# Running sums of the later modulation, 1024 columns wide, and the second gate in the first stream

## The chip, the cores and the metric

The kernel runs on one core of one Trainium2 chip. The metric is the device time of one execution in microseconds (us): the median of the runs shown, 1925.47 us. The profile is of one execution, and its own times are counted from the first to the last instruction (the span). The engines are TensorE (PE, whose weight loads are listed as PEld), VectorE (DVE), ScalarE (ACT), GpSimd (POOL) and SyncE (SP, which here issues nearly all DMAs).

## The reference

Two layers over a sequence of 512 rows with 2048 features, all in float32. Each layer is modulated by a conditioning vector `c`:

```python
c_act = silu(c)
for l in range(2):
    shift, scale, gate = split(c_act @ w_mod[l] + b_mod[l], 3)
    h = x * (1 + scale) + shift
    if l == 0:                       # differential attention, 8 heads, ALiBi
        y = diff_attention(h, a_w_in, a_w_out, ...)
    else:                            # forgetting attention, 16 heads
        sh, sc = split(c_act @ kv_w_mod + kv_b_mod, 2)
        k, v, zf = split((x * (1 + sc) + sh) @ kv_w, ...)
        F = cumsum(log_sigmoid(zf + b_f))
        y = forgetting_attention(h, b_w_in, b_w_out, k, v, F)
    x = layer_norm(ALPHA * x + gate * y, ln_g[l], ln_b[l])
```

`w_mod[l]` is 2048 x 6144 and `kv_w_mod` 2048 x 4096. So beside the large products there are vector-matrix products whose weights must all be read once: shift and scale of layer 0, its gate, shift and scale of the shared keys and values, and shift, scale and gate of layer 1.

## The kernel before

**Matmuls.** A float32 product is made of three TensorE products of a high and a low part (`products`, lines 208 to 210). The weights come as tiles of 128 x 2 x 512 (`wst`), are cast on ACT to the high part (`whi`, L113), and DVE subtracts to get the low part (`wlo`, L114). `WeightStream` loads them up to four tiles ahead and has two or three split tiles ready. A `group` is one job of 512 output columns: 8 weight tiles, and for each of them 4 bursts (one for each of four accumulators in PSUM) of 6 matmuls. After the last weight tile each accumulator is evicted by ACT and DVE (`evac`), and the next group takes the same four accumulators. Jobs come in this order: the start (the first heads, under an order written out by hand), then for heads 2 to 7 a query/key group (`qk`) and a value/gate group (`vg`), the output projection of layer 0 (`oA`, 4 groups), the shared values (`vj`, 5 groups), the shared keys (`kj`, 4 groups), layer 1's query/gate groups, and its output projection. What stands in `pieces` (attention of the head before, built from small closures) is taken up one piece per burst, in `tick`.

**The sums.** The vector-matrix products of the later modulation are not made on TensorE. DVE keeps a running sum: for each block of 128 rows, `macc = w * cact + macc` over 512 columns (L433; the first block L431), with `cact` as a scalar for each partition. After 16 blocks the sum still has to be added over the 128 partitions: a 32 x 32 transpose (L464) and a reduction (L465) on DVE, and once for each vector a small matmul (L474), an add of the bias, and a store to DRAM.

**Background and ticks.** The generator `mod_stream` makes one step of a sum for each `next`. `tick` calls it after a burst as often as the group's `bg` says. So the spread of ticks over bursts sets how densely the sums stand among the other work. There are two streams:

- the first (pool `ap`): gate of layer 0 (4 segments of 512 columns) and the shared keys' and values' shift and scale (8 segments). Each load is 128 x 2 x 512, 512 KB, two steps' worth, in two buffers. It runs from group `qk[2]` to `vg[7]`.
- the second (pool `npool`, made in `open_n`): shift and scale (8 segments) and gate (4 segments) of layer 1. Each load is 128 x 512, 256 KB, in three buffers, and steps 50 to 105 use tiles of the pool `kpool` and are loaded 8 ahead. It runs in groups 1 and 2 of `oA`, in `vj[1]` to `vj[4]` and in all of `kj`.

The results come back through DRAM: `fold(0)` in the first group of `oA`, `fold(1)` 9 bursts into `kj[2]`, and the gates are broadcast (`row_bcast`) in the output projections.

**Order.** After the start, a planner gives each engine its list of instructions at build time, from its own costs and from the dependencies; the steps of the sums are kept in program order among themselves. Each engine then works through its list in order, and so does the DMA queue of SP.

Of the kernel before, what the change touches and what calls it, by code (L numbers as in the profile page):

```python
# [10 lines left out]
F32 = mybir.dt.float32  # L11
# [3 lines left out]
ALU = mybir.AluOpType  # L15

P = 128
D = 2048
# [126 lines left out]
def tile_yoco(  # L145
# [250 lines left out]
    def mod_stream(segs, new_stage, new_acc, nk, deep=range(0), new_deep=None):  # L396

        todo = [(i, r) for i in range(len(segs)) for r in range(KT // nk)]  # L400
        loaded = {}
        summed = []

        def load(k):
            i, r = todo[k]
            src, col, _ = segs[i]
            t = new_deep() if k in deep else new_stage()
            rows = src[nk * r * P : nk * (r + 1) * P, col : col + 512]
            nc.sync.dma_start(t, rows.rearrange("(k p) n -> p k n", p=P) if nk > 1 else rows)
            loaded[k] = t  # L410

        def load_upto(k):
            n = len(loads)
            while n < len(todo) and n <= (k + 7 if n in deep else k + 2 // nk):
                load(n)
                loads.append(n)
                n += 1

        loads = []
        load_upto(-1)  # L420
        for k, (i, r) in enumerate(todo):
            load_upto(k)
            if r == 0:
                acc = new_acc()
            t = loaded.pop(k)
            for kk in range(nk):
                kt = nk * r + kk
                w = t[:, kk, :] if nk > 1 else t

                if kt == 0:  # L430
                    ins = V.tensor_scalar(acc, w, cact[:, 0:1], None, op0=ALU.mult)  # L431
                else:
                    ins = V.scalar_tensor_tensor(acc, w, cact[:, kt : kt + 1], acc, op0=ALU.mult, op1=ALU.add)  # L433
                tc.keep_in_program_order(ins)
                if kt == KT - 1:
                    summed.append(segs[i][2](acc))
                if kt in (1, 9) and summed:
                    if next(summed[0], None) is None:
                        summed.pop()
                yield  # L440
        for n, _ in enumerate(summed[0]):

            for _ in range(1 if n else 6):
                yield
# [375 lines left out]
    segs = []  # L820
    fours = four_ones(ap)
    for dst, src, col, bias, one in (
        (gate_dram[0], w_mod[0], 2 * D, b_mod[0], (0.0,)),
        (mod_dram[0], kv_w_mod, 0, kv_b_mod, (0.0, 1.0)),
    ):
        n = len(one)
        steps = mod_rows(ap, fours, dst, bias[col : col + n * D], one)
        segs += [(src, col + 512 * f, partial(steps, f)) for f in range(4 * n)]
    background = mod_stream(
        segs,  # L830
        lambda: ap.tile([P, 2, 512], F32, name="ms", tag="ms", bufs=2),
        lambda: ap.tile([P, 512], F32, name="macc", tag="macc", bufs=2),
        2,
# [264 lines left out]
    group(qk[2], False, lambda b, acc: keep(("qk", b), acc), bg=lambda k: k % 3 == 2)  # L1098
# [41 lines left out]
    group(vg[2], True, keep_vg, bg=lambda k: k % 2)  # L1140
    for h in range(3, A_HEADS):
# [16 lines left out]
        group(qk[h], False, evac, bg=lambda k: k % 2)  # L1158
# [11 lines left out]
        group(vg[h], True, evac_rest, bg=lambda k: 1 if k % 8 in (1, 3, 4, 5, 7) else 0, after_sub=early if h == A_HEADS - 1 else None)  # L1170
# [17 lines left out]
    def out_projection(jobs, layer, zp, opened, residual, norm, after_held=None):  # L1188
# [10 lines left out]
        for k, (f, job, banks) in enumerate(jobs):  # L1199
# [54 lines left out]
            bg = (lambda n: 1 if n % 3 else 0) if layer == 0 and k in (1, 2) else 0  # L1254
# [7 lines left out]
    def open_n():  # L1262
        nonlocal background
        actx.close()
        pool = nctx.enter_context(tc.tile_pool(name="npool", bufs=1, reuse_waits="tile"))
        zp.extend((pool, pool.tile([P, TB, D], F32, name="n"), pool.tile([P, TB, 4, 6], F32, name="nstats")))
        fours = four_ones(pool)
        segs = []
        for dst, col, one in ((mod_dram[1], 0, (0.0, 1.0)), (gate_dram[1], 2 * D, (0.0,))):
            n = len(one)  # L1270
            steps = mod_rows(pool, fours, dst, b_mod[1, col : col + n * D], one)
            segs += [(w_mod[1], col + 512 * f, partial(steps, f)) for f in range(4 * n)]
        background = mod_stream(
            segs,
            lambda: pool.tile([P, 512], F32, name="ms", tag="ms", bufs=3),
            lambda: pool.tile([P, 512], F32, name="macc", tag="macc", bufs=2),
            1,

            deep=range(50, 106),
            new_deep=lambda: ktile("msk"),  # L1280
        )
# [560 lines left out]
```

## Time and profile before

| | |
|---|---|
| runs of the kernel | 1925.35, 1925.47, 1926.13 us |
| span of the profiled execution | 1923.5 us, 2.0 us below the median of the runs (its time with what lies around the span is not listed) |
| PE busy | 1910.4 us (99%), 8921 matmuls |
| DVE busy | 1370.3 us (71%) |
| ACT busy | 732.9 us (38%) |
| granted TensorE clock | 0.999 |
| DMA | 382.22 MB, mean 199 GB/s |
| steps of the sums on DVE (L433, L431) | 360 and 24, 512 columns each |
| loads of the sums issued on SP (L409) | 168 + 64 + 56 |

How to read it: "busy" is the time in which an engine has work in hand, as a share of the span. Matmuls overlap, so each is listed with 0.39 us while in the chain of waits one follows the other after 0.23 us. In the lists a tile is named by its program name (`macc<-ms,cact,macc`), L433 is line 433 of the kernel, and what stands after `<-` in brackets or behind a bar is what ended an engine's idle time.

### The profile page before, as it was taken

How to read it: one execution, taken by the hardware profiler on the slowest of the kernel's cores; microseconds unless marked ns; L12 is line 12 of the kernel's file. 1: busy time of each engine (PE TensorE's matmuls, PEld its weight loads, DVE VectorE, ACT ScalarE, POOL GpSimd, SP SyncE). 2: the span in 40 equal slices, each digit the busy share in tenths (PEclk: the TensorE clock that was granted, in tenths of full speed). 3: DMA queues.
4: the chain of work that ended last, by engine and by line, in shares of the span. 5: the costliest groups of instructions: out<-in, count | busy, mean ns of one | idle time of the engine just before them, and what ended most of it. 6: DMA issues, size and time to landing. Idle time of an engine off the chain costs nothing.

```text
span 1923.5 us, 25879 instructions
## 1 busy us (share of the span) xinstructions
PE 1910.4 (99%) x8921; PEld 1593.5 (83%) x8921; DVE 1370.3 (71%) x2617; ACT 732.9 (38%) x1266; POOL 2.3 (0%) x11
## 2 busy tenths in 40 slices
PE   8999999999999999999999999999999999999998
PEld 7888888888888888888888898888888888888887
DVE  8993578777676868667675477777566666686768
ACT  3656344333232344521272232224344444453122
POOL 0000000000000000000000000000000000000000
PEclk9999999999999999999999999999999999999999
DMA  9993566676767675476557586775355555555622
GB/s 346 385 333 95 160 186 196 213 234 196 228 203 224 207 223 180 122 241 222 179 165 256 181 294 211 258 258 160 114 149 156 161 149 160 154 154 170 224 93 110
DMA packets 352275, 382.22 MB, mean 199 GB/s; under 512 B 77912, under 2 KB 256244, under 8 KB 351376
## 3 DMA queue, kind: packets, MB, share of 16 engines
q1 hardware_dynamic: 349040, 376.23, 62.2%
q10 hardware_dynamic: 3104, 4.35, 0.6%
q8 instruction: 70, 1.15, 0.3%
q14 instruction: 61, 0.50, 0.1%
HBM read 348.68 MB, written 31.80 MB: 198 GB/s over the span
## 4 chain that ended last, share of the span: by engine, by line
PE 97%; DVE 1%; SPq 1%; DMA 0%; issue 0%; ACT 0%; ACTq 0%
PE acc L208 27%; PE acc L210 27%; PE acc L209 27%; PE acc L720 4%; PE sc L720 2%; PE sc L210 1%; PE sc L209 1%; PE sc L208 1%; PE o L208 1%; PE o L210 1%; PE o L209 1%; PE o L720 1%; SPq L568 0%; PE tr L686 0%; PE tr L660 0%; DMA sms<-in_w_mod_dram 0%
## 5 line engine op out<-in xcount | busy, mean ns | idle before, releaser
L113 ACT CAST whi<-wst 128x1024 fp32r<-128x1024 f32 (+2 forms) x298 | 303.4, 1018 | 617.6 <-PE acc L210 310.1
L114 DVE TENSOR_TENSOR wlo<-wst,whi 128x1024 fp32r<-128x1024 f32 (+2 forms) x298 | 351.4, 1180 | 248.8 <-ACT whi L113 228.9
L208 PE MATMUL acc<-hh,whi 128*128 128x512 f32 x1184 | 462.9, 391 | 0.0
L209 PE MATMUL acc<-hl,whi 128*128 128x512 f32 x1184 | 461.6, 390 | 0.0
L210 PE MATMUL acc<-hh,wlo 128*128 128x512 f32 x1184 | 460.0, 390 | 0.0
L208 PE MATMUL acc<-whi,hh 128*128 128x512 f32 (+1 forms) x1104 | 418.5, 379 | 0.0
L209 PE MATMUL acc<-wlo,hh 128*128 128x512 f32 (+1 forms) x1104 | 416.7, 377 | 0.0
L210 PE MATMUL acc<-whi,hl 128*128 128x512 f32 (+1 forms) x1104 | 416.2, 377 | 0.0
L433 DVE SCALAR_TENSOR_TENSOR macc<-ms,cact,macc 128x512 f32<-128x512 f32 x307 | 229.0, 746 | 63.0 <-DMA ms<-in_w_mod_dram 44.5
L210 PEld LDWEIGHTS acc<-hh,wlo 128*128 128x128 f32 x1184 | 222.3, 188 | 47.4
L208 PEld LDWEIGHTS acc<-hh,whi 128*128 128x128 f32 x1184 | 222.3, 188 | 44.0 <-DVE sgb L1509 0.8
L209 PEld LDWEIGHTS acc<-hl,whi 128*128 128x128 f32 x1184 | 222.5, 188 | 42.3
L210 PEld LDWEIGHTS acc<-whi,hl 128*128 128x128 f32 x1104 | 207.3, 188 | 38.9
L208 PEld LDWEIGHTS acc<-whi,hh 128*128 128x128 f32 x1104 | 207.3, 188 | 37.2 <-DVE ztmp L1241 0.6
L209 PEld LDWEIGHTS acc<-wlo,hh 128*128 128x128 f32 x1104 | 207.4, 188 | 36.0
L618 DVE SCALAR_TENSOR_TENSOR sacc<-sms,cact,sacc 128x512 f32<-128x512 f32 (+1 forms) x128 | 89.9, 703 | 4.6 <-DMA sms<-in_w_mod_dram 0.7
L904 ACT ACTIVATE e<-e,mn 128x128 f32<-128x128 f32 (+3 forms) x64 | 36.0, 563 | 109.5 <-DVE mn L900 102.9
L1559 ACT ACTIVATE eb<-eb,mnb 128x128 f32<-128x128 f32 (+1 forms) x64 | 35.9, 561 | 72.7 <-DVE mnb L1556 72.4
L720 PE MATMUL acc<-wlo,hh 128*128 128x512 f32 x128 | 49.8, 398 | 0.0
L720 PE MATMUL acc<-whi,hl 128*128 128x512 f32 x128 | 49.3, 393 | 0.0
L720 PE MATMUL acc<-whi,hh 128*128 128x512 f32 x128 | 49.2, 393 | 0.0
L132 DVE TENSOR_TENSOR wlo<-wst,whi 128x768 fp32r<-128x768 f32 (+1 forms) x32 | 34.8, 1088 | 17.8 <-ACT whi L125 16.5
(336 smaller groups left out, 2096.6 us busy)
## 6 DMA issues: line engine op xcount, KB each, us to landing
wst<-in_a_w_in_dram SPq DMA_DIRECT2D x240, 256.0 KB
ms<-in_w_mod_dram SPq DMA_DIRECT2D x136, 256.0 KB
ms<-in_kv_w_mod_dram SPq DMA_DIRECT2D x64, 512.0 KB
wst<-in_b_w_in_dram SPq DMA_DIRECT2D x128, 256.0 KB
sms<-in_w_mod_dram SPq DMA_DIRECT2D x56, 512.0 KB
wst<-in_kv_w_dram SPq DMA_DIRECT2D x56, 512.0 KB
ms<-in_w_mod_dram SPq DMA_DIRECT2D x32, 512.0 KB
wst<-in_a_w_out_dram SPq DMA_DIRECT2D x32, 512.0 KB
```

What stands on the lines that cost most here:

```text
L113: self.nc.scalar.copy(hi[:, :, :w], st[:, :, :w])
L114: self.nc.vector.tensor_tensor(lo[:, :, :w], st[:, :, :w], hi[:, :, :w].bitcast(F32), op=ALU.subtract)
L132: self.nc.vector.tensor_tensor(lo[:, :, :w], st[:, :, :w], hi[:, :, :w].bitcast(F32), op=ALU.subtract)
L208: PE.matmul(dst, lhs[0], rhs[0], start=start, stop=False, skip_group_check=True)
L209: PE.matmul(dst, lhs[0], rhs[1], start=False, stop=False, skip_group_check=True)
L210: PE.matmul(dst, lhs[1], rhs[0], start=False, stop=stop, skip_group_check=True)
L433: ins = V.scalar_tensor_tensor(acc, w, cact[:, kt : kt + 1], acc, op0=ALU.mult, op1=ALU.add)
L618: V.scalar_tensor_tensor(acc, w, sc, acc, op0=ALU.mult, op1=ALU.add)
L720: PE.matmul(bank[n, bk], l, r, start=start, stop=stop, skip_group_check=True)
L904: S.activation(e[:, :w], e[:, :w], AF.Exp, bias=mn, scale=-1.0, accum_out=rs)
L1559: S.activation(e[:, :w], e[:, :w], AF.Exp, bias=mn, scale=-1.0, accum_out=rs)
```

## The change

- `mod_stream` now works on 1024 columns with one accumulator and one 512 KB load (128 x 1024) per step, two buffers, one load ahead; the deep prefetch is gone. After a segment's 16 steps come two steps of their own for the two transposes and reductions; five empty steps stand before the last vector's matmul.
- Layer 1's gate moves from the second stream to the first, between layer 0's gate and the shared shift and scale.
- The ticks (`bg`) are spread anew in each group.

```diff
-    def mod_stream(segs, new_stage, new_acc, nk, deep=range(0), new_deep=None):
...
+    def mod_stream(segs, new_stage, new_acc, ahead):
+
+        todo = [(i, kt) for i in range(len(segs)) for kt in range(KT)]
+        loaded, turned_sums = [], []
 
         def load_upto(k):
...
+            while len(loaded) < min(k + 1, len(todo)):
+                i, kt = todo[len(loaded)]
+                src, col, _ = segs[i]
+                loaded.append(new_stage())
+                nc.sync.dma_start(loaded[-1], src[kt * P : (kt + 1) * P, col : col + 1024])
+
+        for k, (i, kt) in enumerate(todo):
+            load_upto(k + ahead)
+            w, one = loaded[k], cact[:, kt : kt + 1]
+            loaded[k] = None
+            if kt == 0:
                 acc = new_acc()
...
+                ins = V.tensor_scalar(acc, w, one, None, op0=ALU.mult)
+            else:
+                ins = V.scalar_tensor_tensor(acc, w, one, acc, op0=ALU.mult, op1=ALU.add)
+            tc.keep_in_program_order(ins)
+            if kt == 4:
+                while turned_sums:
+                    next(turned_sums.pop(0), None)
+            yield
+            if kt == KT - 1:
+                for half, steps in enumerate(segs[i][2]):
+                    turned_sums.append(steps(acc[:, 512 * half : 512 * half + 512]))
+                    next(turned_sums[-1])
+                    yield
+        for _ in range(5):
+            yield
+        for steps in turned_sums:
+            next(steps, None)
...
     background = mod_stream(
...
+        vectors(
+            ap, (
+                (gate_dram[0], w_mod[0], 2 * D, b_mod[0], (0.0,)), (gate_dram[1], w_mod[1], 2 * D, b_mod[1], (0.0,)),
+                (mod_dram[0], kv_w_mod, 0, kv_b_mod, (0.0, 1.0)),
+            ),
+        ),
+        lambda: ap.tile([P, 1024], F32, name="ms", tag="ms", bufs=2),
+        lambda: ap.tile([P, 1024], F32, name="macc", tag="macc", bufs=1),
+        1,
     )
...
-    group(qk[2], False, lambda b, acc: keep(("qk", b), acc), bg=lambda k: k % 3 == 2)
+    group(qk[2], False, lambda b, acc: keep(("qk", b), acc), bg=lambda k: k % 4 == 3)
...
-    group(vg[2], True, keep_vg, bg=lambda k: k % 2)
+    group(vg[2], True, keep_vg, bg=lambda k: k % 3 == 1)
...
-        group(qk[h], False, evac, bg=lambda k: k % 2)
+        group(qk[h], False, evac, bg=lambda k: k % 3 == 1)
...
-        group(vg[h], True, evac_rest, bg=lambda k: 1 if k % 8 in (1, 3, 4, 5, 7) else 0, after_sub=early if h == A_HEADS - 1 else None)
+        group(vg[h], True, evac_rest, bg=lambda k: k % 2, after_sub=early if h == A_HEADS - 1 else None)
...
-            bg = (lambda n: 1 if n % 3 else 0) if layer == 0 and k in (1, 2) else 0
+            bg = (lambda n: n % 4 == 1) if layer == 0 and k in (1, 2) else 0
...
         background = mod_stream(
...
+            vectors(pool, ((mod_dram[1], w_mod[1], 0, b_mod[1], (0.0, 1.0)),)),
+            lambda: pool.tile([P, 1024], F32, name="ms", tag="ms", bufs=2),
+            lambda: pool.tile([P, 1024], F32, name="macc", tag="macc", bufs=1),
             1,
-
-            deep=range(50, 106),
-            new_deep=lambda: ktile("msk"),
         )
...
-        group(vj[g], True, evac_v(g), bg=lambda k: k % 2)
+        group(vj[g], True, evac_v(g), bg=lambda k: k % 4 == 1)
...
-            kj[g], False, evac_k(g), bg=lambda k: 1 if k % 4 else 0,
+            kj[g], False, evac_k(g), bg=lambda k: k % 2,
```

`vectors` is a new helper that makes the segments of the vectors it is given, each with two transposing halves, through the unchanged `mod_rows`.

More of the change, by code (lines that the diff above doesn't have):

```diff
@@ L393, in cols @@
         return const.tile([P, KT], F32, name=name)
-    def mod_stream(segs, new_stage, new_acc, nk, deep=range(0), new_deep=None):
[L400 to L410, printed above, removed]
-        def load_upto(k):
[L413 to L423, printed above, removed]
-                acc = new_acc()
[L425 to L444, printed above, removed]
@@ L819, in tile_yoco, with vectors @@
     ap = actx.enter_context(tc.tile_pool(name="ap", bufs=1, reuse_waits="tile"))
[L820 to L828, printed above, removed]
-    background = mod_stream(
[L830 to L833, printed above, removed]
+    def vectors(pool, wanted):
+        fours = four_ones(pool)
+        segs = []
+        for dst, src, col, bias, one in wanted:
+            n = len(one)
+            steps = mod_rows(pool, fours, dst, bias[col : col + n * D], one)
+            segs += [(src, col + 1024 * f, (partial(steps, 2 * f), partial(steps, 2 * f + 1))) for f in range(2 * n)]
+        return segs
+    background = mod_stream(
+        vectors(
[7 more added lines that the diff above has]
+        1,
     )
```

9 lines of the change are left out of this document (removed).

## Prediction

> **What bounds the kernel now.** I read the page's first and fourth parts first (busy time of each engine, and the chain that ended last).
>
> ```profile
> PE 1910.4 (99%) x8921; PEld 1593.5 (83%) x8921; DVE 1370.3 (71%) x2617; ACT 732.9 (38%) x1266; POOL 2.3 (0%) x11
> ...
> PE 97%; DVE 1%; SPq 1%; DMA 0%; issue 0%; ACT 0%; ACTq 0%
> ```
>
> TensorE's matmuls are the chain for 97% of the span, and the change adds or removes no matmul of weight: each of the four vectors still ends in one small matmul (L474). So the change can act on the time only through gaps in the matmul stream. Next I read the waits, by who waited for whom: those of the weight loads (PEld) from 200 to 1346 us, where both streams of sums run, DVE's from 208 to 785 us, SP's from 208 to 1346 us, and ACT's over the whole span.
>
> ```profile
> PEld o L210 <- DVE al L955: 0.7, 3, 0.2
> PEld sc L1339 <- ACT n L1314: 0.6, 1, 0.6
> ...
> DVE macc L433 <- DMA ms<-in_kv_w_mod_dram: 15.4, 13, 2.8
> ...
> SPq L409 <- DVE macc L433: 178.8, 161, 6.4
> ...
> ACT whi L113 <- PE acc L210: 310.1, 98, 6.8
> ```
>
> Columns: total us, times, longest. The longest wait of the weight loads is 0.7 us in all; the stretch has nearly nothing left to win. The weight casts (L113) wait 310.1 us for TensorE to give buffers back, so the split weights stand ready well ahead. The sums wait for their own loads (15.4 us in 13 waits), and SP's issues of those loads wait for the sums (178.8 us): a loop of two buffers. Busy times by stretch:
>
> ```profile
> 200.00:1346.00 1146.00, 1145.77 (x5414) 958.73 (x5413) 825.61 (x1573) 410.34 (x704) 0.00 (x0) 1.00 0.67 209
> ...
> 260.00:310.00 50.00, 49.98 (x235) 41.77 (x234) 42.15 (x105) 22.66 (x47) 0.00 (x0) 1.00 0.68 195
> 310.00:360.00 50.00, 50.00 (x236) 41.86 (x235) 43.11 (x111) 20.98 (x48) 0.00 (x0) 1.00 0.66 201
> ...
> 455.10:501.20 46.10, 46.10 (x214) 38.57 (x213) 31.22 (x54) 12.87 (x20) 0.00 (x0) 1.00 0.75 234
> ...
> 1206.00:1250.00 44.00, 44.00 (x197) 36.45 (x196) 31.31 (x41) 10.69 (x12) 0.00 (x0) 1.00 0.78 256
> ```
>
> After the stretch's length come busy us of PE, PEld, DVE, ACT and POOL, the granted clock, the DMA share and GB/s. PE is busy 1145.77 of 1146 us; DVE has slack everywhere, least at 260 to 360 us (42.15 and 43.11 of 50).
>
> **The change, part by part.**
>
> *The sums.* Prices, from the groups of instructions with shapes kept apart:
>
> ```profile
> L433 DVE SCALAR_TENSOR_TENSOR macc<-ms,cact,macc 128x512 f32<-128x512 f32 x307 | 229.0, 746 | 63.0 <-DMA ms<-in_w_mod_dram 44.5 <-DMA ms<-in_kv_w_mod_dram 15.4
> L433 DVE SCALAR_TENSOR_TENSOR macc<-msk,cact,macc 128x512 f32<-128x512 f32 x53 | 39.7, 749 | 1.0
> L431 DVE TENSOR_SCALAR macc<-ms,cact 128x512 f32<-128x512 f32 x21 | 10.0, 478 | 2.5 <-DMA ms<-in_kv_w_mod_dram 2.1 <-DMA ms<-in_w_mod_dram 0.4
> L464 DVE STREAM_TRANSPOSE mturn<-macc 128x512 f32<-128x512 f32 x24 | 16.9, 706 | 0.3
> L465 DVE TENSOR_REDUCE mred<-mturn 128x16 f32<-128x512 f32 x24 | 16.3, 679 | 0.3
> L1751 DVE SCALAR_TENSOR_TENSOR z<-z,lrstd,ln_b 128x1024 f32<-128x1024 f32 x6 | 7.4, 1281 | 0.1
> L1315 DVE TENSOR_SCALAR n<-n,mv,lrstd 128x1024 f32<-128x1024 f32 x4 | 3.2, 808 | 0.0
> ```
>
> Now 360 accumulations at 746 to 749 ns and 24 first products at 478: 268.7 + 11.5 = 280.2 us. After, 180 at 1.281 us (L1751 is the same form, in place, 1024 wide) and 12 at 0.808: 230.6 + 9.7 = 240.3 us. The 24 turns and reductions (33.2 us) stay. DVE loses 39.9 us of work, all of it off the chain: 0.
>
> *The spread.* First stream: before 12 segments of 16 steps and a tail of 6, 198 of 206 ticks; after 8 segments of 16 + 2 steps and a tail of 5, so 150 of 154 ticks, 128 of them with a wide operation. Second: 78 steps of 112 ticks. By stage on DVE: a gate/value stage (the stretch from 455.1) goes from 20 to 16 ticks, 31.22 - 20 x 0.746 + 16 x 1.281 = 36.8 of 46.1 us; the stage from 260 from 16 to 11, 42.15 - 11.9 + 14.1 = 44.3 of 50; the one from 310 likewise 45.3 of 50. The key stages, after which nothing on DVE evicts, go from 24 to 16 ticks: 31.31 - 17.9 + 20.5 = 33.9 of 44. So the first stream's stages become fuller though the sum falls.
>
> *Loads.* The first stream's tile stays 512 KB, but it feeds one tick instead of two. A gate/value stage moved 20 x 262 KB for the sums and will move 16 x 524 KB: 234 - 114 + 182 = 302 GB/s, by the row's 0.75 at 234 GB/s a DMA share of 0.97 (estimate; 4 KB rows may cost less than 2 KB ones). SP issues 192 such loads instead of 288, never on the chain. A load that waits for its buffer keeps behind it, on SP, the next weight load and the attention's sends. Second stream: the deep prefetch in K buffers goes; the key stages' demand is 256 - 24 x 262 KB / 43.6 us + 16 x 524 KB / 43.6 us = 304 GB/s. What hides a late sum there is the lead of the weights; its bound is 0 to +2 us, and I take 0.
>
> *The second gate.* It is read only by the last projection, after 1700 us, so no one waits: 0. Modulation 1 is now ready at tick 78 of the 80 that end with the second key group, and its fold stands 9 bursts later: some 15 us for one matmul, one add, a store and a load of 16 KB. Even at the 5.2 us of the slowest big load below, twice that fits. I take 0, up to +2.
>
> *Where a late DVE is felt at once.* At the border of a gate/value stage the next group needs the four accumulators back. DVE's timeline at the first such border, then the chain of waits there:
>
> ```profile
> 404.90 0.75 DVE L433 SCALAR_TENSOR_TENSOR macc<-ms,cact,macc 128x512 f32<-128x512 f32 x1
> 405.56 0.41 DVE L866 SCALAR_TENSOR_TENSOR sg<-th,acc 128x256 f32<-128x256 f32 x1
> 405.89 0.74 DVE L433 SCALAR_TENSOR_TENSOR macc<-ms,cact,macc 128x512 f32<-128x512 f32 x1
> 406.56 0.75 DVE L204 TENSOR_TENSOR vl<-acc,vh 128x256 fp32r<-128x256 f32 x2
> 407.60 1.22 DVE L114 TENSOR_TENSOR wlo<-wst,whi 128x1024 fp32r<-128x1024 f32 x1 [0.29 <-ACT whi L113]
> 408.74 0.74 DVE L866 SCALAR_TENSOR_TENSOR sg<-th,acc 128x256 f32<-128x256 f32 x2
> ...
> 409.15 0.23 PE acc L209
> 409.38 0.39 PE acc L208
> 409.77 0.23 PE acc L209
> ```
>
> The third and fourth evictions (L866) end at 409.15 and 409.48, and the matmul at 409.38 takes 0.39 us instead of 0.23: TensorE already waits 0.16 us. DVE's only reserve is the 0.29 us before the low-part split at 407.60. There are four such borders (406, 501, 596, 691 us); after the last gate/value stage the sums are done. Two wide operations instead of three narrow ones stand in the way: 2 x 1.281 - 3 x 0.746 = +0.32 us, less 0.29 idle, so about 0.1 us per border if all is on time. If the load of the operation at burst 29 is late by its longest wait now (2.8 us) it is +2.8. Bounds per border: -0.16 (the wait gone) to +2.8; I take +0.3, near the on-time price: +1.2 us for four.
>
> The other place is the attention of heads 0 and 1, in the two fullest stretches:
>
> ```profile
> 302.61 0.56 DVE L955 TENSOR_TENSOR al<-e,ah 128x384 fp32r<-128x384 f32 x1
> ...
> 303.22 0.39 PE o L210
> ```
>
> The split ends at 303.17 and the matmul that reads it starts at 303.22: here TensorE waits for DVE, three times, 0.7 us in all. Each stretch gets 2.2 us more of DVE work. Bounds: -0.7 (the waits gone) to +4.4 (all of it seen). I take +0.8, nearer the low end, since DVE still idles 5 us in each.
>
> Sum: +1.2 + 0.8 = +2.0 us on a span of 1923.5; what lies around it (2.0 us to the median of 1925.47, the runs shown being 1925.35 to 1926.13) is untouched. 1927.5 us.
>
> **The rivals.**
>
> *The sums fall behind their loads (slower).* Two buffers: a load is issued when the operation before last ends, so one operation costs half of (issue to data + 1.28 us). A gate/value stage gives a tick each 46.1 / 16 = 2.88 us; the limit is passed when issue to data exceeds 4.48 us. SP, DVE and ACT in the stage from 455:
>
> ```profile
> 477.06 0.36 SPq L409 DMA_DIRECT2D ms<-in_kv_w_mod_dram  x1
> 480.11 0.37 SPq L409 DMA_DIRECT2D ms<-in_kv_w_mod_dram  x1
> 486.88 0.37 SPq L409 DMA_DIRECT2D ms<-in_kv_w_mod_dram  x1
> ...
> 480.93 1.54 DVE L433 SCALAR_TENSOR_TENSOR macc<-ms,cact,macc 128x512 f32<-128x512 f32 x2 [0.85 <-DMA ms<-in_kv_w_mod_dram]
> 482.38 1.22 DVE L114 TENSOR_TENSOR wlo<-wst,whi 128x1024 fp32r<-128x1024 f32 x1
> 485.30 1.54 DVE L433 SCALAR_TENSOR_TENSOR macc<-ms,cact,macc 128x512 f32<-128x512 f32 x2 [1.70 <-DMA ms<-in_kv_w_mod_dram]
> 491.23 0.75 DVE L433 SCALAR_TENSOR_TENSOR macc<-ms,cact,macc 128x512 f32<-128x512 f32 x1 [1.80 <-DMA ms<-in_kv_w_mod_dram]
> ...
> 479.68 1.05 ACT L113 CAST whi<-wst 128x1024 fp32r<-128x1024 f32 x1 [4.38 <-PE acc L210]
> ```
>
> Where DVE really waited, issue to data was 480.93 - 477.06 = 3.87, 485.30 - 480.11 = 5.19 and 491.23 - 486.88 = 4.35 us: mean 4.47, on the limit, at a DMA share that is to rise. The written order does not foresee it: the split at 482.38 stood behind a waiting sum though its cast had ended at 480.73. With 5.2 us throughout, an operation costs 3.24 us and DVE ends the stage 16 x 0.36 = 5.8 us late; half of that, less the reserve, is 2.4 us of TensorE per border: 4 x 2.4 + 0.8 = +10.4 us, 1936 us. Against it: two late operations in a row are made up wherever DVE waits for ACT or TensorE, and today's waits (15.4 us) left no mark on PE. The Trainium skill ("DMA: Bandwidth & Descriptors", Anatomy of one DMA) fits one DMA of the GpSimd path as 2.0 us plus bytes at 436 GB/s; that would give, as an estimate, 3.2 us for 512 KB, so 2.24 us per operation, no lag, and a sum of only some +0.4 us for the borders; the rows, 3.87 us at the least with other loads in the queue, differ, and they decide.
>
> *The dense stretch pays (slower).* If the added 4.4 us at 260 to 360 us reach the matmuls whole: +1.2 + 4.4, 1931 us. For it: the matmul at 303.22 already waits. Against: 5 us of idle in each.
>
> *Faster.* If the lighter key stages and projection and the late order took out nearly every wait of 200 to 1346 us: 4 to 5 us, 1921 us. Against: the waits listed above come to little over 1 us.
>
> *Nothing is felt.* 1925.5 us; it lies in the forecast's own range.
>
> **How the numbers follow.** Forecast (two small terms, 1924.2 to 1929.3 us): 0.53. Sums behind their loads: 0.34. Dense stretch: 0.09. Faster: 0.04. What a measurement can tell from no change is about 0.2%, 3.9 us. So faster 0.04, same 0.53, slower 0.34 + 0.09 = 0.43. The range leaves out below 1924.2 the faster case and a little more, and above 1937 the upper third of the load rival: 1924.2 to 1937.
>
> **What would show it.** Right: L433 1024 wide at 1.28 us, 180 of them; DVE some 40 us less busy; at the four borders a matmul after L866 late by 0.1 to 0.5 us; PE still on 97% of the chain. The load rival: L433 waiting for DMA well over today's 63 us, the DMA share in gate/value stages above 0.9, PE gaps of 1 us and more just after 406, 501, 596 and 691 us. Dense stretch: weight loads waiting for al (L955) by microseconds before 380 us. Wrong altogether: a new wait in the key stages (L1300, L1444) or the projection, which I cost at nothing.

## The result, and the profile after

The changed kernel takes 1939.53 us (median of 1934.16 to 1940.25), the kernel before 1925.80 us on the same chip: ratio 1.0067, interval 1.0052 to 1.0081. It is slower by 13.7 us. The forecast of 1927.5 us and its range are both missed; the time is nearest to that of the rival in which the sums fall behind their loads.

The changed kernel's lines are shifted: the wide sum is L416 (L433 before), its load on SP L406 (L409), attention's splits L945 and L946 (L954, L955), the write and the reads of a turned tile L927 and L935 (L936, L944), the gate's eviction L857 (L866), the forget gate's columns L1426 (L1444). First the page: busy times, the chain that ended last, the group of wide sums.

```profile
PE 1916.5 (99%) x8921; PEld 1593.8 (82%) x8921; DVE 1331.3 (69%) x2425; ACT 730.3 (38%) x1266; POOL 2.3 (0%) x11
...
PE 85%; DVE 6%; DMA 5%; issue 1%; SPq 1%; ACT 1%; DVEq 0%; ACTq 0%
...
L416 DVE SCALAR_TENSOR_TENSOR macc<-ms,cact,macc 128x1024 f32<-128x1024 f32 x180 | 230.2, 1279 | 69.7 <-DMA ms<-in_w_mod_dram 46.9
```

DVE has lost 39.0 us of work, as priced, but the chain is no longer TensorE's alone: DVE and DMA stand on 11% of it. The busy times of the two streams' stretches, of the kernel before and then of the changed one (columns as in the prediction), show which stretch it is:

```profile
208.00:785.00 577.00, 576.99 (x2676) 481.64 (x2675) 436.19 (x940) 221.98 (x423) 0.00 (x0) 1.00 0.68 205
785.00:1400.00 615.00, 614.78 (x2950) 515.68 (x2949) 415.80 (x696) 205.64 (x312) 0.00 (x0) 1.00 0.63 205
```

```profile
208.00:785.00 577.00, 568.71 (x2612) 469.18 (x2610) 449.46 (x868) 209.49 (x404) 0.00 (x0) 1.00 0.75 229
785.00:1400.00 615.00, 613.69 (x2942) 515.15 (x2941) 350.79 (x541) 207.59 (x314) 0.00 (x0) 1.00 0.55 178
```

TensorE idles 8.3 us in the first stream's stretch and gets 64 matmuls less done. A matmul is listed with 0.39 us and the next starts 0.23 us after it, so each short gap hides another 0.16 us. Counted by starts, the matmul that stood at 782.5 us before comes 13.9 us later; up to 1184 us another 1.2 us are lost, and nothing after. "Loss" below is always this count against the kernel before. The loss comes in steps, at 306 (0.8 us), 432 (2.9), 570 (1.2) and 724 us (4), and in small ones between. Who waits, first of the weight loads from 200 to 1346 us, then of SP and of DVE from 208 to 785 us, all of the changed kernel:

```profile
PEld o L208 <- ACT ah L945: 12.7, 14, 3.2
PEld o L210 <- DVE al L946: 2.3, 5, 0.9
PEld acc L208 <- issue: 2.1, 5, 0.6
PEld tr L1426 <- issue: 1.5, 1, 1.5
...
SPq L406 <- DVE macc L416: 80.7, 54, 6.3
SPq L935 <- DMA turned<-e: 41.7, 24, 5.8
SPq L406 <- DMA ms<-in_w_mod_dram: 20.4, 15, 2.4
SPq L406 <- DMA ms<-in_kv_w_mod_dram: 13.4, 11, 3.0
...
DVE macc L416 <- DMA ms<-in_kv_w_mod_dram: 22.0, 20, 4.0
DVE macc L416 <- DMA ms<-in_w_mod_dram: 21.7, 22, 2.0
```

The wait that has come is `ah`: the probabilities of attention that came back from DRAM transposed, cast on ACT. It is not in the kernel before's list at all. SP waits longer for the turned tile's write to land (41.7 us against 30.7 before, at L944), and the sums wait 43.7 us for their loads, where it was 22.1 us (15.4 and 6.7). SP's standing for the sums is no longer than before (80.7 us against 108.3); its standing for earlier loads is, 33.8 us against 2.8. One of the steps, the one at 432 us, on SP, DVE, ACT and PE:

```profile
421.17 3.56 SPq L406 DMA_DIRECT2D ms<-in_w_mod_dram  x2
424.78 0.94 SPq L63 DMA_DIRECT2D wst<-in_a_w_in_dram  x2
425.82 0.40 SPq L927 DMA_DIRECT2D turned<-e  x1
427.48 0.34 SPq L406 DMA_DIRECT2D ms<-in_w_mod_dram  x1
...
431.33 1.75 SPq L935 DMA_DIRECT2D e<-turned  x4
...
414.07 1.28 DVE L416 SCALAR_TENSOR_TENSOR macc<-ms,cact,macc 128x1024 f32<-128x1024 f32 x1 [2.05 <-DMA ms<-in_w_mod_dram]
...
417.89 1.28 DVE L416 SCALAR_TENSOR_TENSOR macc<-ms,cact,macc 128x1024 f32<-128x1024 f32 x1 [0.87 <-DMA ms<-in_w_mod_dram]
...
424.62 0.31 DVE L925 STREAM_TRANSPOSE e<-e 128x128 f32<-128x128 f32 x1
...
432.65 1.28 DVE L416 SCALAR_TENSOR_TENSOR macc<-ms,cact,macc 128x1024 f32<-128x1024 f32 x1 [1.25 <-DMA ms<-in_w_mod_dram]
...
435.11 0.28 ACT L945 CAST ah<-e 128x128 fp32r<-128x128 f32 x1
...
435.44 0.39 PE L208 MATMUL o<-vh,ah 128*128 128x256 f32 x1 [2.73 <-ACT ah L945]
```

The same tile in the kernel before, on DVE and SP:

```profile
420.63 0.31 DVE L934 STREAM_TRANSPOSE e<-e 128x128 f32<-128x128 f32 x1
...
420.96 0.34 SPq L936 DMA_DIRECT2D turned<-e  x1
...
424.44 1.98 SPq L944 DMA_DIRECT2D e<-turned  x4
```

Two things make the tile late. First, DVE turns it late: it had stood 2.05 and 0.87 us for the loads of two sums, with attention's steps behind them, and the turn ends at 424.93 instead of 420.94, where TensorE itself is only 0.8 us behind. Second, SP has just put two 512 KB loads of the sums and two weight loads into its queue in one bunch (the second of the big ones had to stand for its buffer; the row of two issues takes 3.56 us); the turned tile's write goes out behind them at 425.82 and the reads, which wait for it, only at 431.33, 5.5 us later (3.5 before). The cast is at 435.11, 10.2 us after the turn (7.0 before), and TensorE, which works through its list in order, stands 2.73 us before the matmul that reads it. So here the turn is 3.2 us later than TensorE's own lag and the trip 3.2 us longer; at 570 us it is 4.3 and 2.5, at 724 us 2.0 and 1.8. Less what TensorE stood, the slack was some 3.7, 5.8 and 1.5 us (an estimate from these rows): at the first two places neither half alone would have used it up. Of the 28 tiles turned between 208 and 790 us, the mean from the turn's end to the cast is 10.3 us (16.4 at most) against 8.8 (12.6) before; 0.7 us of it, against 0.1, passes before SP reaches the write. The Trainium skill ("DMA: Bandwidth & Descriptors", Anatomy of one DMA) says that a DMA's waits for semaphores are made on the issuing sequencer, before dispatch; the rows of SP here agree: a load without a free buffer holds what follows it on SP, 3.56 us for two issues that take 0.34 us each when nothing is waited for.

### The profile page after: what moved, and what is told of

Read it like the earlier page. It is cut to its first block, busy times and chain, and to the rows that moved or that the text cites. A ratio compares the mean times of both kernels' runs of the same rounds, so it can differ in the third digit from the quotient of the medians.

```text
span 1938.5 us, 25447 instructions
## 1 busy us (share of the span) xinstructions
PE 1916.5 (99%) x8921; PEld 1593.8 (82%) x8921; DVE 1331.3 (69%) x2425; ACT 730.3 (38%) x1266; POOL 2.3 (0%) x11
## 4 chain that ended last, share of the span: by engine, by line
PE 85%; DVE 6%; DMA 5%; issue 1%; SPq 1%; ACT 1%; DVEq 0%; ACTq 0%
PE acc L208 23%; PE acc L210 23%; PE acc L209 23%; PE acc L706 5%; PE sc L706 2%; DMA turned<-e 2%; DVE macc L416 1%; DVE wlo L114 1%; DMA e<-turned 1%; PE o L208 1%; PE o L706 1%; PE sc L209 1%; PE sc L208 1%; PE sc L210 1%; PE o L210 1%
## 5 line engine op out<-in xcount | busy, mean ns | idle before, releaser
L416 DVE SCALAR_TENSOR_TENSOR macc<-ms,cact,macc 128x1024 f32<-128x1024 f32 x180 | 230.2, 1279 | 69.7 <-DMA ms<-in_w_mod_dram 46.9
```

Of the source, the lines that this page charges most:

```text
L416: ins = V.scalar_tensor_tensor(acc, w, one, acc, op0=ALU.mult, op1=ALU.add)
```

## The experiments

Three theories were put up, to which the expectations refer: (A) DVE stands in order ahead of its loads, and all that follows it on DVE is late; (B) the loads' bytes and their places on SP delay attention's transfers; (C) DVE has too much to do, or its pieces of 1.28 us are too long. From run 12 on, B is put as two: the theory of the bytes (on their way) and the theory of the standing (of loads on SP, ahead of attention's transfers). Times are medians, with the ratio to the kernel before on the same chip and its interval; losses and waits are of the one profiled execution.

**1. A third buffer, two loads ahead.** In the first stream, room being made by sharing a buffer between `mturn` and `tog` and dropping one of `mred`:

```diff
-        lambda: ap.tile([P, 1024], F32, name="ms", tag="ms", bufs=2),
+        lambda: ap.tile([P, 1024], F32, name="ms", tag="ms", bufs=3),
...
-        1,
+        2,
```

> The changed kernel with three 512 KB buffers and two loads ahead in the first stream (the room comes from letting the small transposing tile share another tile's buffer). Theory A (VectorE, working in order, stands before its own loads because two buffers with one tick's notice are too few, and the attention's steps wait behind it): the waits of L416 for DMA in the first stream (22.0 + 21.7 us from 208 to 785 us) fall below 15 us, the weight loads' wait for ah (12.7 us) below 4 us, time 1926 to 1930 us. Theory B (the loads' bytes and places in SyncE's queue delay the attention's transfers through DRAM, whatever VectorE does): more is queued ahead of them, waits for ah stay at 10 us or grow, time 1936 to 1942 us. Theory C (VectorE has too much to do in the first stream, in pieces of 1.28 us that cannot be interrupted): little change, 1935 to 1940 us.

1933.35 us, 1.0049 [1.0031, 1.0066], between the numbers of A and B; the profiled execution was a late one, 1940.14, and its waits may be larger than usual. The waits for `ah` fall to 4.8 us and DVE's for loads to 14.9, but a new one comes at the borders at 502 and 699 us. Weight loads, then SP at the first of them:

```profile
PEld acc L208 <- issue: 6.9, 2, 4.4
...
494.45 6.65 SPq L1001 DMA_DIRECT2D ogT<-turned_og  x8
501.21 0.38 SPq L406 DMA_DIRECT2D ms<-in_kv_w_mod_dram  x1
```

Here the load came behind eight fetches of attention's turned output that took SP 6.65 us; the sum waited 3.1 us for it on DVE, with the evictions behind. So a single late load can do what the rival feared, but this happens twice and not at each border.

**2. The second gate back in the second stream** (wide there too; the first stream's ticks thinned to every fourth step of the query groups and every third of the gate groups, the value groups' raised from every fourth to every third):

```diff
-                (gate_dram[0], w_mod[0], 2 * D, b_mod[0], (0.0,)), (gate_dram[1], w_mod[1], 2 * D, b_mod[1], (0.0,)),
+                (gate_dram[0], w_mod[0], 2 * D, b_mod[0], (0.0,)),
```

> The changed kernel with the second layer's gate back in the second stream; operations and loads stay 1024 wide, and the ticks of the first stream are thinned to its 114 steps (query/key groups every 4 bursts, gate/value groups every 3), those of the shared values raised to every 3. A and B: a load is asked for every 4.1 to 5.4 us instead of 2.7 to 4.1 us, so the weight loads' wait for ah falls below 3 us; time 1926 to 1929 us. C: VectorE has a quarter less to do there as well, but its operations stay 1.28 us long, so a part of the loss stays, 1928 to 1934 us. If the loss came from the second stream (the wait of 1.3 us near 1189 us), it stays or grows: above 1930 us.

1944.27 us, 1.0099 [1.0084, 1.0114]. The first stretch is whole again (PE 576.94 of 577 us), the second is not:

```profile
785.00:1400.00 615.00, 603.88 (x2873) 505.12 (x2872) 384.82 (x565) 197.43 (x294) 0.00 (x0) 0.99 0.62 200
```

The loss moved with the gate: 6 us in the last, narrow group of values, where TensorE waits for the low parts of the weights (`acc` for `wlo`, 5.6 us), and some 10 us in the first key group (3.5 us more for `wlo`, 3.9 us for L1426, and matmuls at a clock of 0.83 to 0.89 behind these waits). The wide form alone harms nothing where it is thinly spread.

**3. One load for each segment.** All operations stay; 15 of each segment's 16 blocks of weights are left out and the first is used for all.

```diff
+                if once and kt:
+                    loaded.append(loaded[-1])
+                    continue
```

> The changed kernel with one load for each segment of the first stream instead of 16: all 16 operations read the same tile, so the weights of 15 of 16 blocks of rows are left out; VectorE's instructions are the same. A and B (the loads are at fault, by waits or by bytes): the loss is gone, 1923 to 1928 us. C (VectorE's work and its long operations are at fault): the loss stays, 1934 to 1940 us.

1926.63 us, 1.0009 [1.0000, 1.0018].

```profile
208.00:785.00 577.00, 577.00 (x2676) 481.33 (x2675) 463.20 (x884) 221.97 (x423) 0.00 (x0) 1.00 0.42 125
```

DVE does more in this stretch (463.20 us) than in the changed kernel and TensorE never stops. (C) is out: the loss is made by the loads. The profiled execution (1930.71 us) was again a late one: it loses 5.3 us in the first key group, at the forget gate's columns, though the second stream is the changed kernel's.

**4. The first stream's loads issued by GpSimd** instead of SP (`queue.dma_start` with `nc.gpsimd`).

> The changed kernel with the first stream's loads issued from GpSimd, which is idle, instead of SyncE: same bytes, same buffers, but neither the weight loads nor the attention's transfers stand behind a load that waits for its buffer. B in its form of SyncE's order: the waits for ah fall below 4 us, 1926 to 1931 us. A: VectorE waits for its loads as before or longer (40 us and more), 1935 to 1942 us. B in its form of bytes in the DMA engines: 1934 to 1940 us.

1977.63 us, 1.0269 [1.0252, 1.0286], much worse: SP has none of these loads, but the sums wait 54.9 us for them and TensorE 20.6 us at the borders and 19.4 us for `ah`, where B expected under 4.

This can't separate the theories, since the sums wait longer for their loads than in the changed kernel (43.7 us); what makes the loads later on GpSimd was not looked into.

**5. Loads that nobody reads, paced by DVE.** The sums read one fixed tile; each load is held back by a one-column write of DVE into its buffer.

```diff
+                    tc.keep_in_program_order(V.memset(loaded[-1][:, 0:1], 0.0))
...
+                w = fixed
```

> The changed kernel with all loads of the first stream kept, each paced by a one-column memset of VectorE one tick ahead, but read by nobody: the 128 operations read one fixed tile (their sums are wrong by that). So the bytes and SyncE's issues stay, and VectorE no longer stands before its own loads. Theory A (VectorE waiting in order for its loads): the loss of the first stream is gone as without loads, 1925 to 1930 us. Theory B (bytes and queue places delay the attention's transfers): the weight loads still wait for ah by 8 us and more, 1934 to 1941 us.

1943.01 us, 1.0093 [1.0076, 1.0111]. Inconclusive: by the edit the one-column write must wait for the load before it in the same buffer, and DVE still stood 23.3 us ahead of its sums (listed as `issue`, so the profile does not say for what). Run 8 avoids this.

**6. Only the gate moved, 512 wide.** The kernel before with the second gate in its first stream, and ticks in 5 of 8 steps of the query groups and 7 of 8 of the gate groups.

```diff
         (gate_dram[0], w_mod[0], 2 * D, b_mod[0], (0.0,)),
+        (gate_dram[1], w_mod[1], 2 * D, b_mod[1], (0.0,)),
```

> The kernel before with nothing changed but the place of the second layer's gate: summed in the first stream, 512 columns wide and with 512 KB loads for two steps as before, in ticks raised to 5 of 8 bursts in query/key groups and 7 of 8 in gate/value groups (262 steps). If the density of the loads is the cause (A or B): a loss of the same kind and order, 1931 to 1942 us. If the width, the single load ahead or the single accumulator is: no loss, 1925 to 1928 us.

1941.58 us, 1.0079 [1.0064, 1.0094]. A loss of the same size in the same stretch, 16 us (PE 566.77 of its 577 us), without any wide operation. But the waits are others:

```profile
PEld acc L208 <- issue: 6.3, 6, 1.7
PEld o L208 <- ACT ah L955: 5.2, 4, 1.9
PEld o L210 <- DVE al L956: 4.8, 11, 1.3
```

Here the borders and the splits on DVE (`al`) pay more than `ah`; the sums wait 42.0 us for their loads, and attention's trip is no longer than in the kernel before (8.6 us in the mean). It is closer to the form that the rival foresaw. The run also adds 64 sums on DVE (467.22 us busy in the stretch); run 3, at 463.20 us without the loads, loses nothing.

**7. The second gate back, its ticks spread otherwise:** every second step of the projection, every eighth of the narrow value group, every fourth of the first key group.

```diff
-            bg = (lambda n: n % 4 == 1) if layer == 0 and k in (1, 2) else 0
+            bg = (lambda n: n % 2) if layer == 0 and k in (1, 2) else 0
...
+        group(vj[g], True, evac_v(g), bg=(lambda k: k % 8 == 1) if g == 4 else (lambda k: k % 3 == 1))
```

> All sums 1024 wide, but the second layer's gate in the second stream (114 steps in each), and the second stream's ticks spread around the two places that were hurt there: 4 ticks instead of 11 in the narrow last values group, 8 instead of 16 in the first key group with the forget gate's sums, every second burst in the projection. A and B alike: no stage asks for a load more often than every 2.7 us, none of the PE waits of 1 us and more stays, 1924.5 to 1928 us. If 1024-wide operations cost by themselves: 1930 us and more.

1936.27 us, 1.0053 [1.0037, 1.0068]. Nothing is lost in the first stretch, nothing at L1426 (where the first key group has half the ticks), but 8.4 us in the projection and 3.9 in the narrow value group; in the projection the sums wait 21.4 us for their loads (DVE, 860 to 960 us). Three spreads, three places: the loss goes with the 512 KB loads, to where they stand dense or, in the narrow value group with its four ticks, right behind such a place.

**8. Loads that nobody reads, DVE not waiting.** As 5, but the mark that lets a load go is a token of DVE's that GpSimd copies into the load's buffer. All bytes, places and the pace stay; the sums' values are left out.

```diff
+                    tok = fixed[1]()
+                    tc.keep_in_program_order(V.memset(tok, 0.0))
+                    G.tensor_copy(loaded[-1][:, 0:1], tok)
```

> The changed kernel's first stream with every load kept, in bytes, order and pace, but VectorE waits for none of them: the sums read one fixed tile, and before each load VectorE writes a token of one element per partition (four buffers), GpSimd copies it into the load's tile, and the load on SP waits for that copy. If VectorE's standing in order ahead of its loads makes the loss (A), the stretch from 208 to 785 us loses at most 2 us against the kernel before, and the time is 1926 to 1930 us with the 1.3 us of the first key group. If the loads' bytes and their places on SP delay attention's trip through DRAM by themselves (B), the 14 us stay and the time is 1937 to 1943 us, TensorE waiting over 8 us for ah.

1937.68 us, 1.0062 [1.0047, 1.0077]. Up to the end of the first stretch 9.8 us are lost, 1.3 of them already before 208 us, and TensorE still waits for `ah`. Weight loads, then SP:

```profile
PEld o L208 <- ACT ah L954: 9.3, 10, 2.3
...
SPq L410 <- POOL ms L409: 128.4, 102, 6.2
SPq L410 <- DMA ms<-in_kv_w_mod_dram: 34.3, 22, 2.7
SPq L410 <- DMA ms<-in_w_mod_dram: 33.0, 24, 2.6
```

DVE's waits for loads alone are the smaller part: with them gone 2 of 13.7 us go by the medians, and 4 to 6 of 14 by the profiled executions (this one, 1935.79 us, was the fastest of its four). The detour over GpSimd makes SP's standing longer and keeps GpSimd busy for 103 us, which this run can't tell apart.

**9. Only the width.** First stream 1024 wide with the gate of layer 0 and the shared vectors, thin ticks; the kernel before's second stream.

> Only the width: the first stream 1024 columns wide, without the second gate, a tick in every fourth step of the query groups and every third of the gate groups; the second stream is the kernel before's, 512 wide with its 56 early loads. If the loss is one of how densely the loads come, and not of the width (theory of the density), no wait is left in either stream: 1924 to 1927 us. If 1024-column sums of 1.28 us cost by themselves, over 1929 us.

1925.54 us, 0.9999 [0.9990, 1.0009], and 577.00 of 577 us of PE in the stretch. At this spread the width is worth nothing and costs nothing.

**10. The same 96 loads at the changed kernel's ticks.** Against run 9:

```diff
-        group(qk[h], False, evac, bg=lambda k: k % 4 == 3)
+        group(qk[h], False, evac, bg=lambda k: k % 3 == 1)
...
-        group(vg[h], True, evac_rest, bg=lambda k: k % 3 == 1, after_sub=early if h == A_HEADS - 1 else None)
+        group(vg[h], True, evac_rest, bg=lambda k: k % 2, after_sub=early if h == A_HEADS - 1 else None)
```

> As the run with only the width, but with the changed kernel's ticks (every third step of the query groups, every second of the gate groups), so that the same 112 loads come as densely as in the changed kernel and are over after some three quarters of the stretch. If the density makes the loss, it is that of the changed kernel up to there, some 8 to 10 us: 1933 to 1937 us. If the number of the loads in all makes it, as many as before lose nothing: 1924 to 1928 us.

1931.74 us, 1.0029 [1.0019, 1.0040]: 4.7 us lost, with 5.1 us of waiting for `ah`. (The expectation speaks of 112 loads; with one for each block they are 96.) Density alone makes a loss, but less of it than the 8 us that the changed kernel loses up to the same place; the rest of that difference is not explained.

**11. Attention's turned tiles written and read from ACT's queue.**

```diff
-                nc.sync.dma_start(st["t", i], t)
+                nc.scalar.dma_start(st["t", i], t)
```

> The changed kernel with the first layer's turned tiles written and read back from ScalarE's queue instead of SP's, so that no load of the stream stands ahead of them. If the place on SP is what delays the trip (B), TensorE's 12.7 us of waiting for ah fall by more than half and the time is 1931 to 1935 us. If VectorE's lateness makes the loss (A), or the bytes on their way, 1937 to 1942 us; above that if ScalarE's own standing ahead of its transfers is paid.

1973.39 us, 1.0248 [1.0233, 1.0264]. Neither theory's number, but what the expectation names last: the trip is hardly shorter (10.1 us in the mean), and on ACT, which makes the casts and now also issues the transfers in its order, the casts wait 48.0 us for the tiles' reads, where it was 9.2 us.

```profile
PEld o L208 <- ACT ah L945: 35.2, 11, 5.9
```

**12. Half the bytes.** As 8, each load 512 columns wide instead of 1024.

```diff
-                nc.sync.dma_start(loaded[-1], src[kt * P : (kt + 1) * P, col : col + 1024])
+                nc.sync.dma_start(loaded[-1][:, 0:w], src[kt * P : (kt + 1) * P, col : col + w])
```

> The run in which VectorE waits for no load (token through GpSimd, sums reading a fixed tile), with each load of the first stream half as wide: 256 KB instead of 512 KB, as many loads, in the same places and at the same pace. If the bytes on their way make the loss (theory of the bytes), the stretch from 208 to 785 us loses under 3 us of the 9.8 that it lost with whole loads, and the time is 1926 to 1930 us. If the loads' standing on SP ahead of attention's transfers makes it (theory of the standing), most stays: 1933 to 1938 us.

1926.79 us, 1.0006 [0.9996, 1.0015]. Of the 9.8 us of run 8, 2.1 are left (within the stretch, 1.7 of 8.4). SP still stands for the token as long as there, but for loads to land 18 us instead of 67:

```profile
SPq L411 <- POOL ms L409: 134.9, 104, 4.5
SPq L411 <- DMA ms<-in_kv_w_mod_dram: 9.2, 6, 2.6
SPq L411 <- DMA ms<-in_w_mod_dram: 9.0, 12, 1.2
```

**13. A third buffer, still one load ahead.** The changed kernel, whole, with run 1's room for the buffer but the lead of 1 kept.

> The changed kernel, all of it computed, with a third buffer for the first stream's loads and the load still one tick ahead: the load of a tick waits for the sum of three ticks before it instead of two, so SP hardly stands for a buffer, while the bytes, the pace and VectorE's waits for loads stay. Theory of the standing: 1927 to 1932 us, SP's 80.7 us of waiting for macc nearly gone. Theory of the bytes: 1935 to 1941 us.

1928.42 us, 1.0017 [1.0008, 1.0027]: 11 of the 13.7 us are back, with every byte and every tick in its place. DVE's waits for loads in the first stretch fall from 43.7 to 13.7 us. That stretch, and the weight loads:

```profile
208.00:785.00 577.00, 575.47 (x2667) 479.04 (x2666) 456.13 (x878) 217.46 (x417) 0.00 (x0) 1.00 0.73 230
...
PEld o L208 <- ACT ah L945: 3.6, 6, 2.0
```

The same tile as at 432 us above, on SP:

```profile
420.28 0.34 SPq L406 DMA_DIRECT2D ms<-in_w_mod_dram  x1
...
423.99 0.34 SPq L927 DMA_DIRECT2D turned<-e  x1
...
426.20 1.75 SPq L935 DMA_DIRECT2D e<-turned  x4
```

The load goes out some 3 us ahead of the write, not in a bunch against it, and the reads follow the write after 2.2 us instead of 5.5. One expectation fails: SP's standing for sums does not vanish (71.3 us against 80.7). It stands as long, but no longer with attention's transfers behind it: of the 33.8 us of standing put down to loads on their way 7.0 are left, and from a turn's end to its write pass 0.08 us in the mean, as in the kernel before. The whole trip is 9.6 us in the mean, between 8.8 and 10.3.

**14. Run 8 with the token of the tick before.**

> As the run in which VectorE waits for no load (whole loads, sums reading a fixed tile), but each load waits for the token of the tick before: SP does not stand for VectorE unless that is a whole tick late. Theory of the standing: the 9.8 us fall under 4, 1927 to 1932 us. Theory of the bytes: 1934 to 1939 us.

1932.02 us, 1.0033 [1.0022, 1.0044]; 6.2 us lost instead of 9.8 (within the stretch, 5.3 of 8.4). Between the two theories' numbers. 55.8 us of standing for loads to land in the same buffer (two buffers still) remain, and 7.1 us of TensorE for `ah`.

**15. Run 13 with fewer ticks in the first key group,** made up in the value groups 1 to 3.

```diff
-        group(vj[g], True, evac_v(g), bg=lambda k: k % 4 == 1)
+        group(vj[g], True, evac_v(g), bg=(lambda k: k % 3 == 1) if g < 4 else (lambda k: k % 4 == 1))
...
-            kj[g], False, evac_k(g), bg=lambda k: k % 2,
+            kj[g], False, evac_k(g), bg=(lambda k: k % 2) if g else (lambda k: k % 4 == 1),
```

> The run with the third buffer, with the second stream's ticks thinned in the first key group (every fourth step for every second) and made up in the value groups (every third for every fourth, but not in the last, narrow one). If the sums in the first key group make TensorE's wait for the forget gate's columns, that wait of 1.5 us falls under 0.5 us and the time is 1926.5 to 1928 us, 1.0 us less than with the third buffer alone. If the wait comes from the forget gate's own chain, nothing changes: 1928 to 1929 us. If the value groups' denser ticks come late, as where the second gate was summed there, over 1930 us.

1936.42 us, 1.0054 [1.0040, 1.0068]. The wait for L1426 falls from 1.5 to 0.4 us as expected of the ticks, but 5.6 us are lost in the narrow value group, whose ticks were not changed. From 1110 to 1165 us DVE's sums wait 18.4 us for loads (9.8 in run 13), and its splits of the weights only 3.9 us for casts (12.5): its reserve ahead of TensorE is eaten, and the split comes late (`acc` for `wlo` 5.3 us). The second stream still has two buffers; the group before it came to this place with the loop already behind. That this is why was not tried. No version beats the kernel before, and by these two stretches none could by much: it leaves TensorE 0.01 us idle in the first stretch and 0.2 in the second.

## Why the prediction was wrong

**The second gate: 0. This is the step that failed, and with it the loads, put at "never on the chain".** It asked who waits for the gate's result (no one) and not what its loads do where they now run. Run 9 (width without the gate) gives 0, run 6 (the gate without the width) 16 us, run 2 moves the loss away with the gate. 32 more loads of 512 KB in the same stretch, and the denser ticks that they need, make the loss there; the ticks alone, with 96 loads, make 4.7 us of it (run 10).

**Loads: named, and not priced.** The sentence that a load that waits for its buffer "keeps behind it, on SP, the next weight load and the attention's sends" is half of what happens (the other half is that DVE turns the tiles later), but no sum followed: the price of both was 13.9 us, with 12.7 us listed as weight loads waiting for `ah`. What was missing was the slack of that trip: in the kernel before, the tile of the step at 432 us was cast 1.6 us before its matmul. It was read off nowhere, since TensorE's waits for `ah` were zero. The bandwidth that was feared instead did not come near: 302 GB/s and a share of 0.97 were estimated for a gate/value stage, 251 GB/s and 0.82 stand there (457 to 507 us). The loss came at a share of 0.75 over the stretch. Issue to data was 427.48 to 432.65, 5.17 us, as the slowest row of the prediction. (Its "15.4 us" of waits for loads left out 6.7 us for the other weights.)

```profile
457.00:507.00 50.00, 50.00 (x231) 41.50 (x230) 36.64 (x52) 13.76 (x23) 0.00 (x0) 1.00 0.82 251
```

**The borders: +1.2.** Right in size: 2.1 us in five waits, 0.6 at the longest (`acc` for evictions), under the matmuls' overlap in part. The rival that the sums fall behind their loads named the right loop and condition (over 4.48 us from issue to data), and the wrong place: not DVE late at four borders but SP and DVE late for attention, all along. That its price (1936 us) lies near the time is therefore luck; by its own figures, half of 5.8 us less the idle 0.29, it would be 2.6 us per border and not 2.4. Its border stalls came in runs 1, 4, 5 and 6 (5.7 to 20.6 us).

**The dense stretch: +0.8.** Right in size: some 0.8 us are lost from 260 to 360 us. It was looked for at `al` (L946), which is 0.9 us there; another 1.1 us stands one instruction earlier, at `ah`, which was not named.

**The sums: 0.** Right: 180 at 1.279 us for the 1.281 taken, 39.0 us less work for 39.9, and no gain from it.

**The key stages: nothing.** Off by 1.2 us: the forget gate's rows come late on DVE (L1426); runs 7 and 15, with thinner sums there, have 0.4 us of this wait for 1.5. The place varies, though: run 3's execution loses 5.3 us there. The projection is rightly at nothing.

What the runs show of the cause: in the first stream, two buffers of 512 KB, a load for each tick and the load one tick ahead make a loop in which DVE stands for loads, SP for DVE, and loads go out late and in bunches in front of attention's trip through DRAM. Taking DVE's standing away leaves 9.8 of 13.9 us; a third buffer at the same lead leaves 2.0; halving the bytes as well as taking DVE's standing away leaves 2.1. The theories of the bytes and of the standing, put up against each other for runs 12 to 14, both met their numbers in one run each, 12 and 13: they are two factors of one loop, how long a buffer is held and how many there are. Over the 28 tiles, set against TensorE's own lag, the turn comes 0.8 us later than in the kernel before in the changed kernel, and 0.9, 1.1 and 0.8 us later in runs 8, 12 and 13: about the same. The trip is longer by 1.5 and 2.1 us in the changed kernel and run 8, but by 0.8 in run 13 and shorter by 0.5 in run 12. So the trip is what the runs that mend the loss have changed; DVE's lateness uses up the slack; what it would cost alone no run shows. These are means of single executions, and run 6 shows that denser sums without a longer trip can lose as much at other places.

## What to carry to other kernels

When background work is moved, cost its transfers where they will run, not only its result: list what else goes through the same issuing queue there, and how much slack each of those trips has before its reader, also where no wait is seen yet. A ring of two buffers whose load takes nearly two ticks has no reserve; a third buffer at the same lead took back 11 of 13.7 us here, and with a longer lead as well only about 6, since the wait moved to another place. Before costing a gain, look whether the bounding engine has anything to give: here it was idle for 0.2 us in 1192.

## What the runs showed of the hardware

A gap in TensorE's work can cost more than itself. After the gap at 724 us matmuls started 0.43 us apart instead of 0.23. PE around it, then the granted clock (columns: length, PE busy, clock, DMA share, GB/s):

```profile
726.65 0.38 PE L208 MATMUL o<-vh,ah 128*128 128x256 f32 x1 [2.29 <-ACT ah L945]
...
727.47 0.63 PE L208 MATMUL acc<-hh,whi 128*128 128x512 f32 x1
727.89 0.63 PE L209 MATMUL acc<-hl,whi 128*128 128x512 f32 x1
...
724.00:727.00 3.00, 0.71 (x5) 1.00 0.44 89
727.00:731.00 4.00, 4.00 (x13) 0.57 0.97 290
```

Some eight matmuls at about half the rate are 1.6 us beside the 2.29 of the gap. The gap of 2.73 us at 432 had no such tail. Other runs spread wider: seven matmuls at half the rate after 1.89 us (run 8, 342 us, clock 0.59 over 342 to 346 us), none after 3.48 us (run 11, 657 us, clock 1.00 over the next 4 us). The Trainium skill ("TensorE: Matmul & The Clock Gate", What's actually happening) states a half clock after an idle window of about 3.4 us, counted in windows that run freely. The measurements differ: gaps well under 3.4 us, which can't hold such a window wherever it lies, were enough several times and longer ones were not. What decides is not shown by any run.
